# Thin transfers on the GpSimd queue, two weight tiles on the ACT queue, and a new order of the first matmuls, in a decoder-step kernel

## The chip, the cores and the metric

The kernel runs on one core of one Trainium2 chip. The metric is the device time of one execution in microseconds; the median of three timed runs is compared. A core has five instruction queues that run beside each other and wait for one another through semaphores: PE (TensorE, the matrix engine, with its weight loads shown as PEld), DVE (VectorE), ACT (ScalarE), POOL (GpSimd) and SP (SyncE, which computes nothing and here issues transfers). A transfer between device memory (HBM) and the on-chip memory (SBUF) is issued by one of these queues and carried out by 16 DMA engines that the core has. A queue works strictly in order, so what stands in front of an instruction on its queue delays it.

## The reference

One layer of a decoder trunk for 320 tokens (256 of a prompt, and 8 sequences of 8 tokens), with D_MODEL = 2048 and everything in float32:

```python
u = x @ w_in                                              # 2048 x 6680
q, k, v, o_pre, i_pre, f_pre, z, xbc, dt_pre = split_columns(u, SPLIT_SIZES)
h_m, C, n, m = mlstm_mixer(q, k, v, o_pre, i_pre, f_pre, b_i, b_f, m_norm_w, C0, n0, m0)
h_s, S, sconv = ssd_mixer(z, xbc, dt_pre, s_conv_w, s_conv_b, dt_bias, A_log, D_skip, s_norm_w, S0, sconv0)
mix = jnp.concatenate([h_m, h_s], axis=-1) @ w_out        # 2048 x 2048
x = layer_norm(ALPHA * x + mix, ln1_g, ln1_b)
f, fconv = conv_ffn(x, w_up, f_conv_w, f_conv_b, w_down, fconv0)   # 2048 x 11008, 5504 x 2048
x = layer_norm(ALPHA * x + f, ln2_g, ln2_b)
```

The two mixers are recurrences (matrix memory with gates; a state-space model with a short convolution). `conv_ffn` runs a three-tap convolution over the up-projected rows of the tokens, whose last two rows per sequence come in as a state (`state_ffn_conv`) and go out as one (`p_fconv`, `s_fconv`). Outputs are the tokens after the layer and all new states.

## The kernel before, in words

The weights (about 200 MB) pass through SBUF once. `Stream` holds a list of weight tiles in the order of use. A tile is 512 KB, 4 k-tiles of 128 rows by 256 columns. `Stream.load` (its transfers are line L61) issues the next tiles on the SP queue as far as there are free slots: four `raw` slots, and at the very start four more tiles in memory that is used for other things later. `Stream.split_to` writes each quarter of the work as two float32r parts: `hi` on ACT (L74) and `lo = raw - hi` on DVE (L75), five of each ahead. A slot is free again when the `lo` of its last part is done.

`run_groups` issues the products: for every k-tile of a unit of 128 output columns three matmuls of 128x320, `hi` by `XH`, `hi` by `XL` and `lo` by `XH` (all through the helper `mm`, L232). With 4 k-tiles to a quarter a weight tile feeds 24 matmuls. Between the quarters the background work is issued in small steps by `Tasks`: generators that yield an estimated TensorE time in ns before their next step. The order of all queues is written out when the program is built; that estimate alone decides where a step lands among the matmuls.

Three places matter here.

**The start.** `x_load` fetches x and the 128x128 identity on SP. `x_transpose` (through the helper `transpose`, L238) turns a block of x on PE, three transposes to a k-tile, then ACT writes `XH` (L406) and DVE `XL` (L407). Four k-tiles are turned before the first product. `load_small` (L461 to L476) issues 17 thin transfers on SP, norm weights, biases, masks and a convolution state, and about 26 us of PE estimate later transposes some of them. `keep_x` adds `XH` and `XL` on POOL (L420) and multiplies the sums with the gate weights on PE (shown as `bk<-T,T`).

**The out projection.** `out_task` works on each of 16 outputs; its two running sums are additions on POOL (L1390, L1393). `ffn_consts` issues ten transfers on SP: eight of `state_ffn_conv` (L1333), one of the convolution's weights (L1335) and one of its bias (L1336), each 86 partitions wide with rows of 512 bytes; 20 us of estimate later PE transposes them (`bk<-ident,rows`).

**The last down projection.** `fstate` stores the new convolution state in nine transfers on SP (L1516, L1518), `gb_rows` and a line before it load the second norm's weights.

Of the kernel before, what the change touches and what calls it, by code (L numbers as in the profile page):

```python
# [21 lines left out]
class Stream:  # L22
    """Weight tiles: loaded ahead, split into float32r parts hi + lo ahead of the matmuls."""
# [20 lines left out]
    def load(self, upto=None, own=()):  # L44
        """Load ahead, as far as there are slots; own tiles are used before the slots."""
        own = list(own)
        while self.nr < len(self.raws) and (own or self.live < self.RB):
            if upto is not None and self.nr >= upto:
                return
            src = self.raws[self.nr]  # L50
            if own:
                t = own.pop(0)
                self.foreign.add(self.nr)
            else:
                t = self.pool.tile([128, 1024], F32, name=f"raw{self.nr}", tag="raw", bufs=self.RB)
                self.live += 1
            t = t[:, 0:src.shape[1] * src.shape[2]].rearrange("p (k m) -> p k m", m=src.shape[2])
            m = src.shape[2]
            step = m if self.nr else 128
            for c in range(0, m, step):  # L60
                self.nc.sync.dma_start(t[:, :, c:c + step], src[:, :, c:c + step])  # L61
            self.rt[self.nr] = t
            self.nr += 1
# [21 lines left out]
    def get(self, q):  # L85
        self.split_to(q + self.HB - 1)
        return self.got.pop(q)
# [83 lines left out]
def _hybrid_step(ctx, tc, I, O):  # L171
    nc = tc.nc
    V, A, G = nc.vector, nc.scalar, nc.gpsimd
    dma = nc.sync.dma_start
# [32 lines left out]
    class Halves:  # L207
        """16 k-tiles as two tiles of 8, so that the first half is free early."""
# [43 lines left out]
    # ---------------------------------------------------------------- constants  # L252
# [9 lines left out]
    def run_groups(groups, mvh, mvl, kmap, done, budget, before=None, n=NT, mark=None):  # L262
        for us in groups:
            for o in us:
                o.ps = bank()
            for s in range(4):
                for o in us:
# [16 lines left out]
            before = None  # L284
# [4 lines left out]
    def rsqrt(pool, x, eps, shape, step=0):  # L289
        """1 / sqrt(x + eps), elementwise on a small tile; x is overwritten."""  # L290
# [26 lines left out]
    def colbc(dg):  # L317
        """Per-token columns (as diagonals) to a bank with the tokens along the free dim, equal in all partitions."""
# [24 lines left out]
    # ---------------------------------------------------------------- weights in the order of use  # L343
# [30 lines left out]
    # ---------------------------------------------------------------- mixer pool, start  # L374
# [10 lines left out]
    G.memset(ones, 1.0)  # L385

# [70 lines left out]
    def load_small():  # L457
        colsr = mt("T1", [108, 128])
        r = 0
        for name, n in (("ln1_g", 16), ("ln1_b", 16), ("mlstm_norm_w", 8), ("ssm_norm_w", 8)):  # L460
            dma(colsr[r:r + n], I[name][0].rearrange("(k p) -> k p", p=128))  # L461
            r += n
        dma(colsr[48:96], I["ssm_conv_w"][0].rearrange("j (k p) -> (j k) p", p=128))
        dma(colsr[96:108], I["ssm_conv_b"][0].rearrange("(k p) -> k p", p=128))
        dma(gbias[:, 0:4], I["mlstm_b_i"].broadcast_to([128, 4]))
        dma(gbias[:, 4:8], I["mlstm_b_f"].broadcast_to([128, 4]))
        dma(gbias[:, 8:24], I["ssm_dt_bias"].broadcast_to([128, 16]))
        dma(alog, I["ssm_A_log"].broadcast_to([128, 16]))
        dma(bicol, I["mlstm_b_i"].rearrange("o h -> h o"))
        dma(m0, I["state_mlstm_m"][0].rearrange("b h -> h b"))  # L470
        hr = mt("T10", [24, 1536])
        dma(hr, I["state_ssm_conv"][0].rearrange("b r c -> (b r) c"))
        dma(c_tm, I["c_tm"])
        dma(dsk, I["ssm_D"].broadcast_to([128, 16]))
        dma(m01, I["c_m01"])
        dma(sel, I["c_sel"])  # L476
        yield 21000
# [12 lines left out]
    # ---------------------------------------------------------------- gates  # L490
# [14 lines left out]
    def gate_task(pg):  # L505
# [23 lines left out]
        # log1p(e) = 2 atanh(e / (2 + e))  # L529
# [31 lines left out]
        # SSD rows  # L561
# [12 lines left out]
        # mLSTM rows  # L574
# [27 lines left out]
        dma(d_s, wd[32:48])  # L602
        dma(d_b, bs[:, 0:NT])
        dma(d_m, M4)
        dma(d_w, ws)
# [13 lines left out]
        dma(O["p_m"][0].rearrange("b h -> h b"), m4[:, 255:256])  # L619
        dma(O["s_m"][0].rearrange("b h -> h b"), ms)  # L620

    # ---------------------------------------------------------------- conv of x, B, C
# [33 lines left out]
    def conv_state():  # L656
# [9 lines left out]
        dma(O["p_sconv"][0].rearrange("b r c -> (b r) c"), so[0:3])  # L666
        dma(O["s_sconv"][0].rearrange("b r c -> (b r) c"), so[3:27])

    # ---------------------------------------------------------------- SSD
# [27 lines left out]
    def ssd_bc():  # L697
        # sample operands: rows (b, term, t); terms x: h l h l, B: h h l l
# [77 lines left out]
    def ssd_sample():  # L776
        """Sample states: products with C for four sequences at a time in column tiles, then the update in place."""
# [185 lines left out]
    # ---------------------------------------------------------------- mLSTM  # L963
# [36 lines left out]
    def ml_setup():  # L1000
        yield from wait("gates", "ssd")
        n0r = mt("T1", [64, 128])
        dma(n0r, I["state_mlstm_n"][0].rearrange("b h (e p) -> (b h e) p", p=128))
# [5 lines left out]
        dma(mbig, I["c_mbig"])  # L1009
# [35 lines left out]
    def ml_prompt_state():  # L1045
# [30 lines left out]
        dma(O["p_n"][0, 0].rearrange("h (e p) -> (h e) p", p=128), po)  # L1076

    def ml_ops():
        """Per head: stacked float32r parts of k * w and v of the samples, and their sum over time."""
# [43 lines left out]
        dma(O["s_n"][0].rearrange("b h (e p) -> (b h e) p", p=128), no)  # L1123
# [183 lines left out]
    run_groups(in_groups, XH, XL, lambda k: k, in_done, 1300, before=start_x, mark="in")  # L1307
# [21 lines left out]
    def ffn_consts():  # L1329
        yield 25000  # L1330
        hr = fr("rows", [86, 16, 128])
        for b in range(8):
            dma(hr[:, 2 * b:2 * b + 2, :], I["state_ffn_conv"][0, b].rearrange("r (i p) -> i r p", p=128))  # L1333
        wr = fr("rows", [86, 4, 128])
        dma(wr[:, 0:3, :], I["ffn_conv_w"][0].rearrange("j (i p) -> i j p", p=128))  # L1335
        dma(wr[:, 3, :], I["ffn_conv_b"][0].rearrange("(i p) -> i p", p=128))  # L1336
# [117 lines left out]
    # ---------------------------------------------------------------- conv FFN  # L1454
# [50 lines left out]
    def fstate():  # L1505
# [10 lines left out]
        dma(O["p_fconv"][0, 0].rearrange("r (i p) -> i r p", p=128), r[:, 0:2, :])  # L1516
        for b in range(8):
            dma(O["s_fconv"][0, b].rearrange("r (i p) -> i r p", p=128), r[:, 2 * b + 2:2 * b + 4, :])  # L1518
# [36 lines left out]
    def gb_rows():  # L1555
        """The norm's g and b as float32r rows g hi, g lo, g hi, b hi, b lo."""
# [5 lines left out]
        for h in range(2):  # L1562
            s = slice(1024 * h, 1024 * h + 1024)
            t = fr("rx", [5, 1024])
            dma(t[0:3], I["ln2_g"][:, s].broadcast_to([3, 1024]))
            dma(t[3:5], I["ln2_b"][:, s].broadcast_to([2, 1024]))
# [11 lines left out]
    for j in range(3):  # L1578
# [13 lines left out]
        if j == 2:  # L1592
            fin["r01"], r2g = fr("big", [128, 2, D]), fr("big", [128, 2, D])
            fin["r2"], fin["g"] = r2g[0:64, 0, :], r2g[:, 1, :]
            dma(fin["g"], I["ln2_g"].broadcast_to([128, D]))
# [10 lines left out]
    # ---------------------------------------------------------------- second norm  # L1606
    # y = (r g) rs + (g nb + b), with the second term from the tensor engine: nb in two parts times the rows of gb_rows.
# [57 lines left out]
def _constants():  # L1665
    """Identity, causal masks and the cumulative-sum matrix (prompt anchored at token 128, sample per sequence)."""
# [49 lines left out]
```

## Time and profile before

| what | value |
|---|---|
| median of 3 runs | 1589.42 us (1588.61 to 1590.03) |
| span of the profiled execution, first to last instruction | 1583.8 us |
| median less span (launch, what lies around the span) | 5.6 us |
| PE busy | 1550.8 us, 98% of the span |
| DVE, ACT, POOL busy | 969.4, 776.3, 241.8 us |
| bytes moved, mean rate | 253.87 MB, 160 GB/s |
| mean granted TensorE clock | 0.990 |

A row of the timeline reads: start in us, duration in us, engine, line of the kernel, operation, written tile `<-` read tiles with their shapes, and how many neighbours were merged (`x8`). In brackets stands how long the engine had been idle before it and what ended that. Rows of "SPq" are the SP queue issuing a transfer; they last as long as the issue keeps the queue, not as long as the bytes take. The page gives one execution its span and no run time of its own, so the span is set against the median by the 5.6 us of the table.

### The profile page before, as it was taken

The numbers are of one execution on the slowest core, as the hardware profiler recorded it, in microseconds if no ns is written. First come the engines' busy times: TensorE is split into PE (matmuls) and PEld (weight loads), VectorE is DVE, ScalarE is ACT, GpSimd is POOL, SyncE is SP. The second block draws the span as 40 slices with busy tenths as digits, with TensorE's granted clock in tenths as the row PEclk, the third lists the DMA queues.
The fourth block names the chain that finished last, engine by engine and source line by source line (L and its number), as shares of the span: only waits on it lengthen the run. The fifth ranks groups of instructions, "written<-read, shape, count | busy, mean of one in ns | idle before, by whom it ended". The sixth has DMA issues, their size and how long they took to land.

```text
span 1583.8 us, 27952 instructions
## 1 busy us (share of the span) xinstructions
PE 1550.8 (98%) x10533; PEld 1500.2 (95%) x10533; DVE 969.4 (61%) x1957; ACT 776.3 (49%) x1533; POOL 241.8 (15%) x548
## 2 busy tenths in 40 slices
PE   8999999999999989999999999999999999999896
PEld 7999889998889989999999999999999999999896
DVE  4775445655677566687777545655644555656565
ACT  4665333444546435566665435555533555555332
POOL 2212110023301033232331000000000000000001
PEclk9999999999999999999999999999999999999998
DMA  8646665466774625454444454454444445454352
GB/s 220 205 140 160 195 193 172 139 185 198 229 231 150 208 91 192 131 155 150 147 148 141 146 163 151 135 158 147 147 153 154 147 147 160 147 150 164 122 160 79
DMA packets 267523, 253.87 MB, mean 160 GB/s; under 512 B 15987, under 2 KB 262207, under 8 KB 267260
## 3 DMA queue, kind: packets, MB, share of 16 engines
q1 hardware_dynamic: 267388, 252.09, 51.6%
q8 instruction: 82, 1.34, 0.3%
q14 instruction: 53, 0.43, 0.1%
HBM read 231.63 MB, written 20.43 MB: 159 GB/s over the span
## 4 chain that ended last, share of the span: by engine, by line
PE 89%; issue 6%; SPq 3%; DMA 1%; DVE 1%; POOL 0%; ACT 0%; POOLq 0%; ACTq 0%; DVEq 0%
PE bk L232 87%; PE bk L238 2%; SPq L1333 1%; DMA T<-w_in 1%; SPq L445 0%; DMA raw<-w_out 0%; DMA T<-state_ssm_conv 0%; SPq L61 0%; POOL big L1644 0%; SPq L1336 0%; DVE big L1379 0%; DVE lo L75 0%; SPq L1335 0%; SPq L461 0%; DVE big L1383 0%
## 5 line engine op out<-in xcount | busy, mean ns | idle before, releaser
L75 DVE TENSOR_TENSOR lo<-raw,hi 128x512 fp32r<-128x512 f32 (+2 forms) x800 | 551.3, 699 | 420.2 <-ACT hi L74 418.4
L74 ACT ACTIVATE hi<-raw 128x512 fp32r<-128x512 f32 (+2 forms) x800 | 486.4, 616 | 474.3 <-PE bk L232 418.9
L232 PE MATMUL bk<-big,hi 128*128 128x320 f32 (+1 forms) x2752 | 609.3, 310 | 0.0
L232 PEld LDWEIGHTS bk<-big,hi 128*128 128x128 f32 x2752 | 462.3, 188 | 0.2
L232 PE MATMUL bk<-big,lo 128*128 128x320 f32 (+1 forms) x1376 | 426.5, 310 | 0.0
L232 PE MATMUL bk<-XH,hi 128*128 128x320 f32 x832 | 269.2, 324 | 0.0
L232 PEld LDWEIGHTS bk<-big,lo 128*128 128x128 f32 x1376 | 259.3, 188 | 0.0
L232 PE MATMUL bk<-XH,lo 128*128 128x320 f32 x832 | 258.0, 310 | 0.0
L232 PE MATMUL bk<-XL,hi 128*128 128x320 f32 x832 | 257.9, 310 | 0.0
L232 PE MATMUL bk<-HH,hi 128*128 128x320 f32 x688 | 215.2, 313 | 5.0 <-ACT hi L74 5.0
L232 PE MATMUL bk<-HH,lo 128*128 128x320 f32 x688 | 213.5, 310 | 0.0
L232 PE MATMUL bk<-HL,hi 128*128 128x320 f32 x688 | 213.3, 310 | 0.0
L232 PEld LDWEIGHTS bk<-XH,hi 128*128 128x128 f32 x832 | 157.1, 189 | 14.4 <-issue 4.6
L232 PEld LDWEIGHTS bk<-XL,hi 128*128 128x128 f32 x832 | 157.3, 189 | 0.2
L232 PEld LDWEIGHTS bk<-XH,lo 128*128 128x128 f32 x832 | 157.1, 189 | 0.0
L232 PEld LDWEIGHTS bk<-HH,hi 128*128 128x128 f32 x688 | 130.0, 189 | 5.2 <-ACT hi L74 5.2
L1482 DVE SCALAR_TENSOR_TENSOR c<-c,fcol,c 128x336 f32<-128x336 f32 x172 | 98.0, 570 | 58.3 <-ACT c L1480 55.3
L232 PEld LDWEIGHTS bk<-HH,lo 128*128 128x128 f32 x688 | 129.8, 189 | 0.2 <-DVE lo L75 0.2
L232 PEld LDWEIGHTS bk<-HL,hi 128*128 128x128 f32 x688 | 129.9, 189 | 0.0
L193 POOL TENSOR_SCALAR fst<-c 128x18 f32<-128x18 f32 x86 | 22.2, 265 | 567.4 <-ACT c L1475 567.4
L232 PE MATMUL bk<-MH,hi 128*128 128x320 f32 x256 | 80.5, 315 | 10.8 <-ACT hi L74 10.8
L232 PE MATMUL bk<-MH,lo 128*128 128x320 f32 x256 | 79.8, 312 | 0.0
(299 smaller groups left out, 1447.3 us busy)
## 6 DMA issues: line engine op xcount, KB each, us to landing
raw<-ffn_w_up SPq DMA_DIRECT2D x172, 512.0 KB
raw<-w_in SPq DMA_DIRECT2D x100, 512.0 KB
raw<-ffn_w_down SPq DMA_DIRECT2D x71, 512.0 KB
raw<-w_out SPq DMA_DIRECT2D x32, 512.0 KB
T<-state_mlstm_C SPq DMA_DIRECT2D x32, 256.0 KB
s_C<-T SPq DMA_DIRECT2D x32, 256.0 KB
T<-state_ssm SPq DMA_DIRECT2D x8, 512.0 KB
s_ssm<-T SPq DMA_DIRECT2D x8, 512.0 KB
```

Of the source, the lines that this page charges most:

```text
L74: nc.scalar.activation(h, src, AF.Copy)
L75: nc.vector.tensor_tensor(l, src, h.bitcast(F32), ALU.subtract)
L193: G.tensor_scalar(out, in_, 1.0, 0.0, ALU.mult, ALU.add)
L232: nc.tensor.matmul(out, lhsT=lhsT, rhs=rhs, start=start, stop=stop)
L238: nc.tensor.transpose(out, in_, ident[b:b + p, b:b + p])
L1333: dma(hr[:, 2 * b:2 * b + 2, :], I["state_ffn_conv"][0, b].rearrange("r (i p) -> i r p", p=128))
L1482: V.scalar_tensor_tensor(c[:, 0:336], xp[:, j:j + 336], fcol[:, j, i:i + 1], c[:, 0:336], ALU.mult, ALU.add)
```

## The change

Five edits. The thin transfers of `load_small`, `gate_task` (its four scratch stores and two outputs), `conv_state`, `ml_setup` (two), `ml_ops`, the prompt's last state, `ffn_consts`, `fstate`, `gb_rows` and the load of the second norm's g go to the POOL queue (`gdma`); transfers of weights, x, the matrix states and the outputs y stay on SP. The first two weight tiles are issued on ACT. Seven 128x128 products of ones by ones, whose result nobody reads, stand at the head of PE. The first four k-tiles of x are no longer turned in one go: the first products stand between the transposes. And the first call of `get` splits one quarter only, no longer five.

```diff
-                self.nc.sync.dma_start(t[:, :, c:c + step], src[:, :, c:c + step])
+                (self.nc.sync if self.nr > 1 else self.nc.scalar).dma_start(t[:, :, c:c + step], src[:, :, c:c + step])
...
     def get(self, q):
-        self.split_to(q + self.HB - 1)
+        self.split_to(q + self.HB - 1 if q else 0)
...
-    dma = nc.sync.dma_start
+    dma, gdma = nc.sync.dma_start, nc.gpsimd.dma_start
...
                     for kk in range(nk):
                         k = k0 + kk
+                        if each is not None:
+                            each(us.index(o), s, kk)
...
     G.memset(ones, 1.0)
+    warm = bank()
+    for _ in range(7):
+        mm(warm[:, 0:128], ones, ones, True, True)
...
-    def x_transpose(c):
-        flags.add(("xt", c))
-        t = box.pop(("x", c))
-        for kk in range(4):
+    def x_transpose(c, kks=range(4)):
+        t = box["x", c]
+        if kks[-1] == 3:
+            flags.add(("xt", c))
+            del box["x", c]
+        for kk in kks:
...
-            if k == 1:
-                st.split_to(0)
...
     def load_small():
+        yield 9000
...
-            dma(colsr[r:r + n], I[name][0].rearrange("(k p) -> k p", p=128))
+            gdma(colsr[r:r + n], I[name][0].rearrange("(k p) -> k p", p=128))
...
-        dma(sel, I["c_sel"])
-        yield 21000
+        gdma(sel, I["c_sel"])
+        yield 17000
...
         if u == s == 0:
-            x_transpose(0)
+            x_transpose(0, [0])
...
+    def each_x(u, s, kk):
+        if u == s == 0 and kk < 3:
+            x_transpose(0, [kk + 1])
...
-            dma(hr[:, 2 * b:2 * b + 2, :], I["state_ffn_conv"][0, b].rearrange("r (i p) -> i r p", p=128))
+            gdma(hr[:, 2 * b:2 * b + 2, :], I["state_ffn_conv"][0, b].rearrange("r (i p) -> i r p", p=128))
...
-            dma(O["s_fconv"][0, b].rearrange("r (i p) -> i r p", p=128), r[:, 2 * b + 2:2 * b + 4, :])
+            gdma(O["s_fconv"][0, b].rearrange("r (i p) -> i r p", p=128), r[:, 2 * b + 2:2 * b + 4, :])
```

Where the instructions stand now (the changed file's lines are up to 10 higher than the old ones):

On SP in the out projection, before: loads of `w_out` into `raw` slots, with the ten transfers of `ffn_consts` (into `rows`) among them.

```order
L61 DMA raw_6529<-w_out 128x4x256
L61 DMA raw_6577<-w_out 128x4x256
L1333 DMA rows_6628<-state_ffn_conv 86x2x128 x8
L1335 DMA rows_6637<-ffn_conv_w 86x3x128
L1336 DMA rows_6637<-ffn_conv_b 86x128
L61 DMA raw_6644<-w_out 128x4x256
```

Now the ten are gone from SP, and stand on POOL between the additions of `out_task`, behind the sixth pair of them (`c_6271` and `c_6272` are the two running sums):

```order
L1400 TENSOR_TENSOR c_6271<-c_6271,big_6268 128x320
L1403 TENSOR_TENSOR c_6272<-c_6272,c_6629 128x320
L1343 DMA rows_6636<-state_ffn_conv 86x2x128 x8
L1345 DMA rows_6645<-ffn_conv_w 86x3x128
L1346 DMA rows_6645<-ffn_conv_b 86x128
L1400 TENSOR_TENSOR c_6271<-c_6271,big_6268 128x320
L1403 TENSOR_TENSOR c_6272<-c_6272,c_6668 128x320
```

What stands behind them on POOL are the remaining additions. On the matrix engine the place of the transposes of `rows` did not move.

On POOL at the start, now: the 17 transfers of `load_small` stand between the last memset and the additions of `keep_x` (`T_51`, `T_52`), which before followed that memset at once. The rows show the first two of the 17 and the last two.

```order
L940 MEMSET sm_201 128x6
L467 DMA T_49_291<-ln_g 16x128
L467 DMA T_49_291<-ln_b 16x128
...
L481 DMA T_18_130<-c_m 128x448
L482 DMA sel<-c_sel 128x128
L425 ISA
L425 TENSOR_TENSOR T_51_344<-XH_162,XL_164 128x640
L425 TENSOR_TENSOR T_52_346<-XH_162,XL_164 128x640
```

So the additions, and the gate products on PE that read them, now come behind 17 issues on POOL.

On PE at the start, now (before, all twelve transposes `ident,T` came first):

```order
L232 MATMUL bk_80<-ones 128x128 x7
L238 MATMUL bk_158<-ident,T_3_89 128x128 x2
L238 MATMUL bk_158<-ident,T_2_88 128x64
L238 MATMUL bk_170<-ident,T_3_89 128x128 x2
L238 MATMUL bk_170<-ident,T_2_88 128x64
L232 MATMUL bk_154<-XH_162,hi_166 128x320
L232 MATMUL bk_154<-XL_164,hi_166 128x320
L232 MATMUL bk_154<-XH_162,lo_167 128x320
L238 MATMUL bk_179<-ident,T_3_89 128x128 x2
L238 MATMUL bk_179<-ident,T_2_88 128x64
```

The products of the first k-tile moved ahead of the transposes of the third, and need `lo_167` from DVE there.

More of the change, by code (lines that the diff above doesn't have):

```diff
@@ L260, in col, with run_groups @@
         return cols[:, i:i + 1]
-    def run_groups(groups, mvh, mvl, kmap, done, budget, before=None, n=NT, mark=None):
+    def run_groups(groups, mvh, mvl, kmap, done, budget, before=None, n=NT, mark=None, each=None):
         for us in groups:
@@ L283, in run_groups @@
                     tasks.pump(budget)
-            before = None
+            before = each = None
     def ktiles(w, k, n, c, m):
@@ L460, in load_small @@
         for name, n in (("ln1_g", 16), ("ln1_b", 16), ("mlstm_norm_w", 8), ("ssm_norm_w", 8)):
-            dma(colsr[r:r + n], I[name][0].rearrange("(k p) -> k p", p=128))
+            gdma(colsr[r:r + n], I[name][0].rearrange("(k p) -> k p", p=128))
             r += n
[L463 to L470, printed above, removed]
-        hr = mt("T10", [24, 1536])
[L472 to L476, printed above, removed]
-        yield 21000
+        gdma(colsr[48:96], I["ssm_conv_w"][0].rearrange("j (k p) -> (j k) p", p=128))
+        gdma(colsr[96:108], I["ssm_conv_b"][0].rearrange("(k p) -> k p", p=128))
+        gdma(gbias[:, 0:4], I["mlstm_b_i"].broadcast_to([128, 4]))
+        gdma(gbias[:, 4:8], I["mlstm_b_f"].broadcast_to([128, 4]))
+        gdma(gbias[:, 8:24], I["ssm_dt_bias"].broadcast_to([128, 16]))
+        gdma(alog, I["ssm_A_log"].broadcast_to([128, 16]))
+        gdma(bicol, I["mlstm_b_i"].rearrange("o h -> h o"))
+        gdma(m0, I["state_mlstm_m"][0].rearrange("b h -> h b"))
+        hr = mt("T10", [24, 1536])
+        gdma(hr, I["state_ssm_conv"][0].rearrange("b r c -> (b r) c"))
+        gdma(c_tm, I["c_tm"])
+        gdma(dsk, I["ssm_D"].broadcast_to([128, 16]))
+        gdma(m01, I["c_m01"])
+        gdma(sel, I["c_sel"])
+        yield 17000
         ps = bank()
@@ L601, in gate_task @@
         yield 9000
[L602 to L605, printed above, removed]
+        gdma(d_s, wd[32:48])
+        gdma(d_b, bs[:, 0:NT])
+        gdma(d_m, M4)
+        gdma(d_w, ws)
         p1 = bank()
@@ L618, in gate_task @@
         yield
-        dma(O["p_m"][0].rearrange("b h -> h b"), m4[:, 255:256])
-        dma(O["s_m"][0].rearrange("b h -> h b"), ms)
+        gdma(O["p_m"][0].rearrange("b h -> h b"), m4[:, 255:256])
+        gdma(O["s_m"][0].rearrange("b h -> h b"), ms)
     XS = mt("T10", [128, 8, NT])
@@ L665, in conv_state @@
         yield
-        dma(O["p_sconv"][0].rearrange("b r c -> (b r) c"), so[0:3])
-        dma(O["s_sconv"][0].rearrange("b r c -> (b r) c"), so[3:27])
+        gdma(O["p_sconv"][0].rearrange("b r c -> (b r) c"), so[0:3])
+        gdma(O["s_sconv"][0].rearrange("b r c -> (b r) c"), so[3:27])
     def ssd_cb():
@@ L1008, in ml_setup @@
         mbig = mt("T2", [128, 448])
-        dma(mbig, I["c_mbig"])
+        gdma(mbig, I["c_mbig"])
         wb = sm([128, 4, 72], name="wb")
@@ L1122, in ml_ops @@
         yield
-        dma(O["s_n"][0].rearrange("b h (e p) -> (b h e) p", p=128), no)
+        gdma(O["s_n"][0].rearrange("b h (e p) -> (b h e) p", p=128), no)
     def ml_chunks():
@@ L1306, in _hybrid_step @@
         tasks.add(t)
-    run_groups(in_groups, XH, XL, lambda k: k, in_done, 1300, before=start_x, mark="in")
+    run_groups(in_groups, XH, XL, lambda k: k, in_done, 1300, before=start_x, mark="in", each=each_x)
     first = []
@@ L1332, in ffn_consts @@
         for b in range(8):
-            dma(hr[:, 2 * b:2 * b + 2, :], I["state_ffn_conv"][0, b].rearrange("r (i p) -> i r p", p=128))
+            gdma(hr[:, 2 * b:2 * b + 2, :], I["state_ffn_conv"][0, b].rearrange("r (i p) -> i r p", p=128))
         wr = fr("rows", [86, 4, 128])
-        dma(wr[:, 0:3, :], I["ffn_conv_w"][0].rearrange("j (i p) -> i j p", p=128))
-        dma(wr[:, 3, :], I["ffn_conv_b"][0].rearrange("(i p) -> i p", p=128))
+        gdma(wr[:, 0:3, :], I["ffn_conv_w"][0].rearrange("j (i p) -> i j p", p=128))
+        gdma(wr[:, 3, :], I["ffn_conv_b"][0].rearrange("(i p) -> i p", p=128))
         yield 20000
@@ L1564, in gb_rows @@
             t = fr("rx", [5, 1024])
-            dma(t[0:3], I["ln2_g"][:, s].broadcast_to([3, 1024]))
-            dma(t[3:5], I["ln2_b"][:, s].broadcast_to([2, 1024]))
+            gdma(t[0:3], I["ln2_g"][:, s].broadcast_to([3, 1024]))
+            gdma(t[3:5], I["ln2_b"][:, s].broadcast_to([2, 1024]))
             yield 6000
```

8 lines of the change are left out of this document (4 added, 4 removed).

## The prediction

> **What bounds the kernel now.** I read the page's head first, then the busy time and granted clock in stretches of 10 us, and then the timeline of each stretch where PE was not full.
>
> ```profile
> span 1583.8 us, 27952 instructions
> PE 1550.8 (98%) x10533; PEld 1500.2 (95%) x10533; DVE 969.4 (61%) x1957; ACT 776.3 (49%) x1533; POOL 241.8 (15%) x548
> 580.00:590.00 10.00, 6.38 (x44) 6.11 (x42) 0.39 (x1) 0.00 (x0) 0.00 (x0) 1.00 0.15 38
> 590.00:600.00 10.00, 2.82 (x10) 2.60 (x11) 2.67 (x4) 3.50 (x8) 1.92 (x2) 0.52 0.81 268
> 628.84 825.17 PE bk L232 x5604
> ```
>
> PE is the bound almost everywhere: what the change does under a full PE is worth nothing, and only the 33 us in which PE is not busy can be won. The stretch rows (busy time of PE, PEld, DVE, ACT, POOL, then clock, DMA share, GB/s) show one hole: from 580 to 600 PE works 9.2 of 20 us. Other holes lie at 1495, in the first 6 us and in the last 20. The change does not touch the last. The last row, from the chain of waits, gives the pace of a full PE: 825.17 / 5604 = 0.147 us for a matmul.
>
> The two holes in the middle, on PE and on ACT, which makes the `hi` that PE waits for:
>
> ```profile
> 586.07 0.31 PE L232 MATMUL bk<-MH,lo 128*128 128x320 f32 x1
> 597.18 0.63 PE L232 MATMUL bk<-MH,hi 128*128 128x320 f32 x1 [10.80 <-ACT hi L74]
> 600.66 0.31 PE L232 MATMUL bk<-MH,hi 128*128 128x320 f32 x1
> 596.50 0.63 ACT L74 ACTIVATE hi<-raw 128x512 fp32r<-128x512 f32 x1 [17.27 <-DMA raw<-w_out]
> 1495.44 0.31 PE L232 MATMUL bk<-HH,lo 128*128 128x320 f32 x1
> 1500.71 0.63 PE L232 MATMUL bk<-HH,hi 128*128 128x320 f32 x1 [4.96 <-ACT hi L74]
> 1505.07 0.32 PE L232 MATMUL bk<-HH,hi 128*128 128x320 f32 x1
> 1500.03 1.98 ACT L74 ACTIVATE hi<-raw 128x512 fp32r<-128x512 f32 x4 [12.78 <-DMA raw<-ffn_w_down]
> ```
>
> ACT waited for a weight tile both times. Why the tile was late stands on the SP queue:
>
> ```profile
> 561.64 6.08 SPq L61 DMA_DIRECT2D raw<-w_out  x2
> 567.77 16.38 SPq L1333 DMA_DIRECT2D rows<-state_ffn_conv  x8
> 584.20 2.31 SPq L1335 DMA_DIRECT2D rows<-ffn_conv_w  x1
> 586.55 3.31 SPq L1336 DMA_DIRECT2D rows<-ffn_conv_b  x1
> 589.96 2.96 SPq L61 DMA_DIRECT2D raw<-w_out  x3
> 1477.57 15.82 SPq L1518 DMA_DIRECT2D s_fconv<-rows  x8
> 1493.51 16.02 SPq L61 DMA_DIRECT2D raw<-ffn_w_down  x8
> ```
>
> Ten thin transfers kept SP from 567.77 to 589.9; then three tiles went out at once, so slots had been free. Eight stores kept it from 1477.57 to 1493.4. The queue was the bound there, while the DMA engines were 15% busy (580 to 590).
>
> **The change, part by part.** The sum is made on the profiled execution, 1583.8 us of span; the median of 1589.42 lies 5.6 us above it, and I take those as unchanged.
>
> *First hole.* With the ten gone from SP, tile loads follow the slots. At 0.147 us the next matmul was due at 586.22 and came at 597.18: 10.96 us. Then 12 matmuls, 597.18 to 600.66, took 3.48 us at the low clock against 12 x 0.147 = 1.76: 1.72 more. Term: -12.7.
>
> *Second hole.* 1495.59 to 1500.71 is 5.12; 15 matmuls to 1505.07 took 4.36 against 2.20: 2.16. Term: -7.3. On POOL the nine stores hold up nobody:
>
> ```profile
> 1446.06 0.11 POOL L1611 MEMSET fsm<- 128x15 f32 x1
> 1574.01 5.15 POOL L1644 TENSOR_TENSOR big<-big,rx 64x512 f32<-64x512 f32 x4 [127.83 <-ACT rx L1643]
> ```
>
> POOL is idle for 127.8 us, and the 14 transfers that now fall in there (norm rows too) fit at any price below 9 us each.
>
> *The price of an issue on POOL* is not in this trace: all its transfers are SP's. The nearest rows:
>
> ```profile
> 26.48 1.07 SPq L461 DMA_DIRECT2D T<-ln_g  x1
> 33.80 0.43 SPq L476 DMA_DIRECT2D sel<-c_sel  x1
> L1333 SPq DMA_DIRECT2D rows<-state_ffn_conv x8: 359/2308/3798, 567.8 to 581.8; - x8
> ```
>
> The 17 of `load_small` took SP 26.48 to 34.23, 0.46 us each; the eight of `state_ffn_conv` took 0.36 at best and 2.31 at the median. So 0.46 to 2.31 for either kind. I take 1.0 for the 17, the middle of the bounds as a ratio, since these very transfers are the low row; and 1.3 for the ten, which carry more rows (172 of 512 bytes each). Nothing excludes the ends.
>
> The Trainium skill ("DMA: Bandwidth & Descriptors", Latency and other measured facts) puts the first byte at about 1 us from the GpSimd queue and 0.6 from SP. Here no run shows the first; by 1.0 us for all 27 the sum would come out the same.
>
> The same page (Issuing engines are not separate DMA queues) speaks against the change: all queues share 16 DMA engines, and issuing from several saves only issue time, usually small beside the transfer. The trace differs: 22 us of issue beside idle DMA engines. By the rule the two terms would be nothing, which is the last rival below; I go by the rows.
>
> *Where POOL's issues could come through to PE.* First the out projection: the ten stand behind the sixth pair of sums, and PE transposes `rows` later.
>
> ```profile
> 0.73 0.45 SPq L393 DMA_DIRECT2D T<-x_prompt  x1
> 571.31 0.91 POOL L1393 TENSOR_TENSOR c<-c,c 128x320 f32<-128x320 f32 x1
> 602.42 0.46 PE L238 MATMUL bk<-ident,rows 86*128 86x86 f32 x4
> ```
>
> That addition is the sixth and ends at 572.2. PE gets to the transposes 24 matmuls behind the hole, without it at 586.22 + 24 x 0.147 = 589.75. Landing takes some 2.5 us (an estimate from the first x tile, 256 KB, issued at 0.73 and used by PE at 4.09, a row further down: 3.4 in all). So 572.2 + 10p + 2.5 must stay under 589.75: p up to 1.5 us is hidden. At 1.3 it is, by 2 us: cost 0. Behind the ten on POOL wait the other sums; what reads those comes after the sixteenth output, and `c` has nine buffers beside the sums, so this costs nothing; if that cover were gone, the price is the 13 us.
>
> Second, the start, where `keep_x`'s additions now stand behind 17 issues:
>
> ```profile
> 2.40 0.10 POOL L934 MEMSET sm<- 128x6 f32 x1
> 7.89 4.06 POOL L420 TENSOR_TENSOR T<-XH,XL 128x640 f32<-128x640 f32 x2 [5.39 <-DVE XL L407]
> 29.72 0.74 PE L232 MATMUL bk<-T,T 128*32 128x320 f32 x8
> ```
>
> POOL is free at 2.5, two additions take 4.06, and PE wants them at 29.7, or 28.7 with what the start gains. 2.5 + 17p + 4.06 stays below that up to p = 1.3. At 1.0 they are done at 23.6: cost 0, with 5 us of cover. The stores of these sums wait on SP with weight loads behind them, in time with the same additions: no further cost.
>
> *The other thin transfers* (states, gate rows, `mbig`) are 12 of about 1 us each, spread from 120 to 540 us, where PE is full and POOL 15% busy overall; four tiles ahead, 14 us of matmuls, hide a late SP row behind them. 0; without cover some 2 us at each.
>
> *The start.*
>
> ```profile
> 4.09 0.66 PE L238 MATMUL bk<-ident,T 128*128 128x128 f32 x2 [4.09 <-DMA ident<-c_ident]
> 5.54 3.10 PE L238 MATMUL bk<-ident,T 64*128 64x64 f32 x10 [0.78 <-DMA T<-x_sample]
> 8.57 0.63 PE L232 MATMUL bk<-XH,hi 128*128 128x320 f32 x1
> 13.51 0.31 PE L232 MATMUL bk<-XH,hi 128*128 128x320 f32 x1
> 16.15 2.31 PE L238 MATMUL bk<-ident,T 128*128 128x128 f32 x12
> 543.43 0.70 PE L232 MATMUL bk<-big,ones 128*128 128x320 f32 x2
> 5.94 0.44 ACT L406 ACTIVATE XH<-bk 128x320 fp32r<-128x320 f32 x1 [3.92 <-PE bk L238]
> 2.97 1.57 SPq L61 DMA_DIRECT2D T<-w_in  x3
> ```
>
> Nothing on PE can start before 4.09, the identity's landing, so the seven products of ones are free: by the row at 543.43 (about 0.55 us for 320 columns at the high clock) 128 columns cost 0.22, or 0.43 at the low clock, 3.0 us for seven, from 0.9 to 4. The three issues on ACT (1.57) fit into its 3.92 idle. What can be won is the slow clock: 18 products took 8.57 to 13.51, 4.9 us, where 18 x 0.147 is 2.6: 2.3. Ten transposes took 3.10, 0.31 each, where twelve later ones took 2.31, 0.19 each: 1.4 for twelve. At most 3.7. On the other side, weight tiles now share the DMA engines with x from the first moment; x_sample, ahead of them so far, may land up to 1 us later. And each early product waits for ACT and DVE (`XH`, then `hi` of 0.63, then `lo`) between transposes, where nothing waited before; if the clock rises no earlier, some 0.8 us are lost. So -3.7 to +1.8; I take -1.0, half the products' part.
>
> The clock rose at 13.5, 4.9 us after the first product, though PE had transposed since 5.5. The Trainium skill ("TensorE: Matmul & The Clock Gate", Part 4: PE-mode transpose) says transposes do not count as busy in the same way; the trace agrees. Its Part 1 asks for about 3.4 us of sustained matmuls: by an estimate from that figure 3.0 us of ones fall just short and the term would be nearer +1 than -1.
>
> Sum: 1583.8 - 12.7 - 7.3 - 1.0 = 1562.8 of span, 1568.4 at the median.
>
> **Rivals.**
> - *POOL is slow for the ten.* At 2.0 us each the transposes wait 572.2 + 20 + 2.5 - 589.75 = 5.0 us, and a pause like that of 1495 costs 2.2 of clock: 1575.6. For it: the 2.31 median. Against: on SP those were back to back, with the first at 0.36. Chance 0.18.
> - *The ten's bytes, not the queue, hold up the tiles of the first hole.* It stays, at 1581.1. For it: the eight got slower after the first (0.36 to 2.31). Against: 15% DMA share, 38 GB/s. Chance 0.04.
> - *POOL at the start.* At 1.6 us each for the 17, the gate products wait 2.5 + 27.2 + 4.06 - 28.7 = 5.1: about 1573.5. Chance 0.06.
> - *Slower than before:* every issue on POOL costs like SP's slow ones, and PE stands behind both groups. The loss is 17p - 22.1 and 10p - 15.0; with 21.0 gained it decides from p = 2.15. At 2.31 it is 17.2 + 8.1 - 21.0 = +4.3: 1593.7. Against: SP issued the 17 at 0.46. Chance 0.04.
> - *The change does not do what it says:* the same DMA engines hold up the tiles at both holes whichever queue issues, and only the start gains: 1588.4. Three tiles went out at once behind the first block, so 0.04.
>
> The forecast has 0.64, with 1565.5 to 1571 of its own (start term -3.7 to +1.8). The range goes up through the two POOL cases: 1565.5 to 1580. Three runs of this kernel spread 0.1%, so 0.2%, 3.2 us, is what a comparison can tell. Faster takes the forecast and the first three rivals: 0.92; slower 0.04; same, the last rival, 0.04.
>
> **What would show it.** No idle row of PE near 586 or 1495, and the clock at 1.00 from 580 to 610; SP's loads of `w_out` 3.5 us apart there; POOL's ten issues ending before 587; the gate products at 28 to 30 without a wait. Products of 0.15 us spacing before 10 us would show the start's term. A wait of PE's transposes for `rows`, or of `bk<-T,T` for POOL, would prove me wrong, and its length is the price I mis-sized.

## The result, and the profile after

| | kernel before | changed kernel |
|---|---|---|
| median of the runs compared, us | 1589.01 (1586.03 to 1590.03) | 1578.95 (1578.14 to 1580.12) |
| ratio, 95% interval | | 0.9945, 0.9933 to 0.9957 |
| profiled execution, span, us | 1583.8 | 1578.3 |

The change gains 10.1 us by the medians; the ratio of 0.9945 puts the gain at 0.55%. The forecast was 1568.4, a gain of 21. The page of the changed kernel, its head:

```profile
span 1578.3 us, 27987 instructions
PE 1553.8 (98%) x10547; PEld 1502.5 (95%) x10547; DVE 976.6 (62%) x1957; ACT 773.1 (49%) x1532; POOL 290.3 (18%) x601
```

PE still fills 98%. The stretches of 10 us show where it does not (after the length of the stretch: busy time of PE, PEld, DVE, ACT, POOL, then granted clock, DMA share, GB/s):

```profile
580.00:590.00 10.00, 10.00 (x70) 10.00 (x69) 7.00 (x12) 5.17 (x10) 10.00 (x7) 1.00 1.03 212
590.00:600.00 10.00, 3.83 (x27) 3.56 (x25) 4.85 (x2) 1.78 (x3) 6.48 (x8) 0.85 1.26 181
600.00:610.00 10.00, 7.91 (x42) 7.90 (x43) 3.86 (x8) 2.38 (x5) 1.19 (x1) 0.64 0.41 114
...
1490.00:1500.00 10.00, 10.00 (x72) 9.99 (x71) 5.94 (x17) 3.49 (x6) 0.00 (x0) 1.00 0.47 150
```

The hole at 1495 is gone. The hole near 590 has only moved by some 7 us, and the DMA share in it is now 1.26 (590 to 600); the old hole began with a share of 0.15. The timeline of the changed kernel there, PE, POOL and the SP queue:

```profile
593.52 0.31 PE L232 MATMUL bk<-MH,lo 128*128 128x320 f32 x1
602.09 0.83 PE L238 MATMUL bk<-ident,rows 86*128 86x86 f32 x4 [8.27 <-DMA rows<-ffn_conv_w]
607.30 0.31 PE L232 MATMUL bk<-MH,lo 128*128 128x320 f32 x1
...
576.06 12.80 POOL L1343 DMA_DIRECT2D rows<-state_ffn_conv  x8
588.85 1.84 POOL L1345 DMA_DIRECT2D rows<-ffn_conv_w  x1
590.69 0.56 POOL L1346 DMA_DIRECT2D rows<-ffn_conv_b  x1
...
583.19 14.26 SPq L61 DMA_DIRECT2D raw<-w_out  x4
```

PE no longer waits for a weight tile. It waits for the thin rows themselves: POOL has issued the last of the ten by 591.25, before PE's last product, but `ffn_conv_w` lands 13.2 us after its issue. The DMA view of 560 to 606 gives KB and the median time from issue to landing:

```profile
raw<-w_out SPq DMA_DIRECT2D x10, 512.0 KB, 8.4
rows<-state_ffn_conv POOLq DMA_DIRECT2D x8, 86.0 KB, 11.4
rows<-ffn_conv_w POOLq DMA_DIRECT2D x1, 129.0 KB, 13.2
```

From the first issue, 576.06, to the last landing, 602.25 in the trace, are 26.2 us. On SP the ten had held the queue for 22.1, and their last packet ended 26.6 us after the first issue (567.77 to 594.35 in the packet records). The time is nearly the same, on another queue. The weight tiles suffer with them: 8.4 us from issue to landing here, against 3.9 at the median of all `w_out` tiles of this kernel.

**Where the 5.4 us between the two spans come from.** The first row of the table is PE's first gate product, the third a product of PE. The others are the split (`lo`) of one and the same weight tile, in both traces, us:

| place | before | after | shift |
|---|---|---|---|
| gate products, start | 29.72 | 32.57 | +2.85 |
| a tile ahead of the first hole | 575.65 | 578.57 | +2.9 |
| the last product ahead of that hole in the kernel before | 586.07 | 590.00 | +3.93 |
| a tile behind it | 631.18 | 633.24 | +2.05 |
| a tile ahead of the second hole | 1448.18 | 1450.23 | +2.05 |
| a tile behind it | 1542.27 | 1537.02 | -5.25 |

The splits run ahead of PE, so a shift that PE has just taken does not show in them yet. By PE's own products the start costs 2.5 (at 543 in the kernel before). Another 1.4 comes soon behind that, in a stretch with this row of the changed kernel:

```profile
548.10 0.41 PE L232 MATMUL bk<-MH,lo 128*128 128x320 f32 x1 [0.68 <-DVE lo L75]
```

The kernel b_cut below, whose code up to there is that of the kernel before, loses 1.2 at the same place, so the change need not be the cause. The first hole then gives 3.93 - 2.05 = 1.9 and the second 7.3. The first products and what is around them, in the changed kernel on PE and POOL:

```profile
0.99 3.36 PE L232 MATMUL bk<-ones 128*128 128x128 f32 x14 [0.99 <-POOL ones L387]
5.46 0.66 PE L238 MATMUL bk<-ident,T 128*128 128x128 f32 x2 [1.11 <-DMA ident<-c_ident]
7.42 1.27 PE L238 MATMUL bk<-ident,T 64*128 64x64 f32 x4 [1.29 <-DMA T<-x_sample]
8.83 0.64 PE L232 MATMUL bk<-XH,hi 128*128 128x320 f32 x1
9.99 0.93 PE L238 MATMUL bk<-ident,T 128*128 128x128 f32 x3
10.84 0.63 PE L232 MATMUL bk<-XH,hi 128*128 128x320 f32 x1
11.81 0.93 PE L238 MATMUL bk<-ident,T 128*128 128x128 f32 x3
16.82 0.30 PE L232 MATMUL bk<-XH,hi 128*128 128x320 f32 x1
...
32.57 0.75 PE L232 MATMUL bk<-T,T 128*32 128x320 f32 x8
...
2.44 0.68 POOL L467 DMA_DIRECT2D T<-ln_g  x1
8.86 0.54 POOL L473 DMA_DIRECT2D gbias<-ssm_dt_bias  x1 [2.07 <-DMA T<-ln_g]
15.25 3.11 POOL L425 TENSOR_TENSOR T<-XH,XL 128x640 f32<-128x640 f32 x2
```

The identity is there at 5.46 where it was there at 4.09, and `x_sample` is transposed at 7.42, 1.88 later than before, so the first product does not come earlier although only half the transposes stand ahead of it; the other six now stand between the products, 0.85 us for each group of three; and the spacing drops to 0.15 us only at 16.8, not at 13.5. POOL issues the 17 in 0.51 to 0.68 us each and is at its sums by 15.25, so it holds up nothing.

### The profile page after: what moved, and what is told of

It reads as the page before. It is cut to its first block, busy times and chain, and to the rows that moved or that the text cites. A ratio compares the mean times of both kernels' runs of the same rounds, so it can differ in the third digit from the quotient of the medians.

```text
span 1578.3 us, 27987 instructions
## 1 busy us (share of the span) xinstructions
PE 1553.8 (98%) x10547; PEld 1502.5 (95%) x10547; DVE 976.6 (62%) x1957; ACT 773.1 (49%) x1532; POOL 290.3 (18%) x601
## 4 chain that ended last, share of the span: by engine, by line
PE 86%; issue 7%; DMA 2%; POOL 1%; DVE 1%; ACT 1%; POOLq 0%; SPq 0%; DVEq 0%; ACTq 0%
PE bk L232 84%; PE bk L238 2%; DMA rows<-ffn_conv_w 1%; POOL T L425 1%; DMA raw<-w_out 1%; DVE lo L75 1%; DMA T<-ln_g 0%; DMA gbias<-ssm_dt_bias 0%; DMA xT<-T 0%; POOL big L1654 0%; ACT hi L74 0%; DVE big L1393 0%; DVE big L1389 0%; ACT L657 0%; ACT T L644 0%
```

## Experiments on the first hole

Theory A says that the ten transfers run over few DMA engines. Rivals: POOL's queue is slow by itself (B); the weight tiles set the stop (C).

**r_cut: the same rows, cut at partition 80.**

```
-        for b in range(8):
-            gdma(hr[:, 2*b:2*b+2, :], state_ffn_conv[0, b] "r (i p) -> i r p")
-        gdma(wr[:, 0:3, :], ffn_conv_w) ; gdma(wr[:, 3, :], ffn_conv_b)
+        for s in (slice(0, 80), slice(80, 86)):
+            gdma(hr[s], state_ffn_conv[0] "b r (i p) -> i (b r) p" [s])
+            gdma(wr[s, 0:3, :], ffn_conv_w [s]) ; gdma(wr[s, 3, :], ffn_conv_b [s])
```

> The changed kernel with the thin loads of ffn_consts still on POOL, the same rows of 512 bytes, but cut by partitions into 80 and 6 (and the eight of state_ffn_conv put together, so six transfers instead of ten). Theory A, few DMA engines: while only these transfers ran in the kernel before, the DMA share was 0.15 of 16 engines, 2.4 engines, and 172 rows took 2.31 us; in the changed kernel they landed at the same pace, 23 us for all, whichever queue issued them. The Trainium skill (DMA: Bandwidth & Descriptors, How many engines) says that the number of partitions decides, 86 giving 2 engines and 80 giving 16. By A the rows land within 5 us of their issue, the 8.27-us wait of PE for rows and the slow clock behind it (together 11.8 us) are gone: about 1567 us, 12 below the changed kernel. Rival B, POOL's queue itself is slow (its issue of 1.59 us, its landing of 11 us): the rows land as late as now, PE waits 6 to 8 us, 1576 to 1579.

Measured: 1568.4 us, ratio 0.9883 (0.9867 to 0.9900), span 1565.4. Its stretch, its timeline (POOL, PE) and its DMA view:

```profile
590.00:600.00 10.00, 10.00 (x74) 9.99 (x73) 8.15 (x14) 5.62 (x11) 3.39 (x4) 1.00 0.59 182
```

```profile
573.94 0.99 POOL L1344 DMA_DIRECT2D rows<-state_ffn_conv  x1
574.93 0.66 POOL L1345 DMA_DIRECT2D rows<-ffn_conv_w  x1
577.38 0.55 POOL L1346 DMA_DIRECT2D rows<-ffn_conv_b  x1
591.53 0.46 PE L238 MATMUL bk<-ident,rows 86*128 86x86 f32 x4
```

```profile
rows<-state_ffn_conv POOLq DMA_DIRECT2D x1, 640.0 KB, 7.7
rows<-ffn_conv_b POOLq DMA_DIRECT2D x1, 40.0 KB, 9.0
```

The wait and the slow clock are gone: the span is 13.0 us shorter than the changed kernel's, and the median 10.6. Of the 13.0, 2.1 stand ahead of the hole already (the product at 586.07 in the kernel before is at 587.86 here, a shift of 1.79 against 3.93); the hole itself accounts for 10.8. B falls: the queue is the same. From the first issue, 573.94, to the last landing, 585.36, are 11.4 us in place of 26.2. The landing in 7.7 to 9.0 us is more than the 5 that A said; that miss costs nothing, since PE comes at 591.5. The packet records show the spread that A needs: in the kernel before, from 576 to 585, on average 2.4 of these packets were in flight and never more than 4; in r_cut, from 574 to 580, 8.2 on average and up to 19. POOL's packets are larger, though, mostly 4 KB where SP's have 512 bytes; the comparison on one queue with one packet size follows with b_cut. The Trainium skill (DMA: Bandwidth & Descriptors, Why a DMA increments its semaphore by 16 and not by 1, on how many engines) says the transfer is split over the largest number up to 16 that divides its partition counts, which makes 2 for 86 and 16 for 80. The 2.4 packets on SP agree; the page names exceptions for some copies from the GpSimd queue, and the packet records do not name the engine.

**r_early: uncut, but issued long before.**

```
-        yield 25000      (ahead of the ten)
+        yield 8000
-        yield 20000      (ahead of their transposes)
+        yield 38500
```

> The changed kernel with the ten thin loads, uncut, issued some 17 to 24 us earlier, the transposes at the same matmul. Theory A, few engines: the ten take 23 us to land from about 552 to 560, so they are there by 584, before PE's transposes at 593.5, and the wait for rows is gone; weight tiles that share their engines land up to 16 us after issue, where four slots cover some 14, so PE may lose 0 to 3 us to hi instead: 1567 to 1570. Rival C, the place of the stop is set by the weight tiles that land late, and the rows are only the last to be seen: PE stops 8 us for hi in place of rows, 1576 to 1579.

Measured: 1576.87 us, ratio 0.9929 (0.9914 to 0.9944). POOL came to them much earlier than I had worked out, 55 us before the changed kernel and not 17 to 24:

```profile
520.76 12.77 POOL L1343 DMA_DIRECT2D rows<-state_ffn_conv  x8 [4.53 <-DVE lo L75]
535.36 0.57 POOL L1346 DMA_DIRECT2D rows<-ffn_conv_b  x1
551.58 1.68 DVE L1376 SCALAR_TENSOR_TENSOR big<-rx,bk 128x320 f32<-128x320 f32 x4 [11.21 <-DMA rx<-xT]
552.17 1.41 PE L232 MATMUL bk<-big,ones 128*128 128x320 f32 x2 [5.20 <-issue]
```

The ten again take 25.2 us from first issue to last landing (545.94), and now the x rows of the first norm (`rx`) land late behind them: DVE waits 11.2 us, PE stops for 5.2 and then runs at the low clock. A had the pace right and the price wrong (0 to 3 us forecast, some 8 measured); C, a stop for `hi`, did not happen either. The stop went to the reader that was due in those 25 us.

**b_cut: the kernel before, all on SP, loads cut as in r_cut and the eight stores of `s_fconv` made two.**

```
+        for s in (slice(0, 80), slice(80, 86)):
+            dma(s_fconv[0] "b r (i p) -> i (b r) p" [s], r[s, 2:18, :])
```

> The kernel before, everything still on SP; only the loads of ffn_consts are cut into 80 and 6 partitions (the eight of state_ffn_conv together, six transfers for ten) and the eight stores of s_fconv are made two in the same way. Theory A, few DMA engines: SP is held for some 3 to 6 us instead of 22 and 16, both holes are gone without any other queue: 1583.8 - 12.7 - 7.3 = 1563.8 of span, about 1569. Rival B2, it is SP as the queue of weight tiles that must not have thin transfers at all (the number of rows counts, 1720 and 1376, not the engines): the holes stay, 1585 to 1589.

Measured: 1567.59 us, ratio 0.9877 (0.9862 to 0.9892), span 1565.4; run again as the base of a later group, 1566.13, 0.9862 (0.9848 to 0.9877). Its SP queue:

```profile
569.31 0.50 SPq L1334 DMA_DIRECT2D rows<-state_ffn_conv  x1
569.86 0.67 SPq L1335 DMA_DIRECT2D rows<-ffn_conv_w  x1
572.01 0.29 SPq L1336 DMA_DIRECT2D rows<-ffn_conv_b  x1
575.85 3.24 SPq L61 DMA_DIRECT2D raw<-w_out  x3
...
1466.69 4.69 SPq L1518 DMA_DIRECT2D s_fconv<-rows  x2
```

SP is held for 3.0 us instead of 22.1, and for 5.1 (with `p_fconv`) instead of about 16. Both holes are gone without any other queue. This is faster than the kernel before and than the changed one. The shift of PE against the kernel before goes from +1.79 (the product at 586.07) to -10.89 (the one at 635.60), which is 12.7, and the tiles then go from -10.88 near 1448 to -18.19 near 1542, which is 7.3: the two terms of the prediction.

On the same queue and with the same packets of 512 bytes, 16.2 are in flight on average (571.5 to 576.2, up to 27) where it was 2.4. All 1720 rows run from their first packet to their last in 4.6 us instead of 24.4.

**f_pool: the changed kernel with its start undone, `load_small` back on SP, loads and stores cut but still on POOL.**

> The changed kernel with its start undone and load_small on SP (both as before), the loads of ffn_consts and stores of s_fconv still on POOL, but cut as in b_cut. If the queue is worth nothing once the transfers are cut: within 0.1% of b_cut, spans within 1 us. If freeing SP is worth something by itself: 1 to 3 us less.

Measured: 1566.65 us, ratio 0.9864 (0.9849 to 0.9878), beside 1566.13 for b_cut on the same chip, with spans of 1564.5 and 1565.7: no difference that these runs can tell. Once the transfers are cut, POOL's queue is worth nothing here. In all these runs the eight transfers of `state_ffn_conv` were merged as well as cut. The transfer of `ffn_conv_w` was only cut: POOL's issue of it fell from 1.84 us to 0.66 and 0.58 for its two pieces, and SP's from 2.31 to 0.67 and 0.52. In the kernel before the last 344 rows, which are those of `ffn_conv_w` and `ffn_conv_b`, took 4.9 us by themselves, more than all 1720 together in b_cut. So the cut alone has this effect; what the merging adds was not measured.

## Experiments on the second hole and on the start

**b_stores: the kernel before, only the nine stores of `fstate` on POOL.**

> The kernel before with only the nine stores of fstate on POOL. By the second term of the prediction, which the changed kernel's trace gives as 7.33 us of shift between the tiles near 1448 and 1542: 1583.8 - 7.3 = 1576.5 of span, about 1582, ratio 0.9954. Rival: the gain there came with the changed order of the rest, 1586 to 1589.

Measured: 1579.99 us, ratio 0.9958 (0.9943 to 0.9973). In its trace the tile shift goes from +4.29 near 1448 to -3.00 near 1542: 7.29, the term of the prediction (the 7.33 in the expectation is 7.30 by the table above). The +4.29 ahead of it is a surprise, since nothing there was edited. In this kernel's trace and in that of the kernel before, from 40 to 46 us:

```profile
40.00:46.00 6.00, 6.00 (x25) 4.50 (x25) 2.35 (x4) 1.58 (x3) 0.00 (x0) 0.50 1.02 354
```

```profile
40.00:46.00 6.00, 6.00 (x45) 5.29 (x44) 2.10 (x4) 2.65 (x6) 1.09 (x2) 1.00 1.04 367
```

Behind 24 transposes that start at 36.8 (36.4 before) the clock is granted at 0.50 in the one execution and at 1.00 in the other. In b_cut's second trace it fell at the same place for 3.4 us. In the other traces it stayed up there, or fell only behind an idle row of PE of 2.2 us or more (s_sp and f_ones below). The same code thus costs up to 3.3 us more or less, from one execution to the next.

**The start, one piece undone at a time.** The changed kernel with the two tiles back on SP (s_sp), with the first tile's transposes in one go (s_block), with `load_small` back on SP (s_small), without the ones (s_noones):

```
s_sp:      -(sync if nr > 1 else scalar).dma_start    +sync.dma_start
s_block:   -x_transpose(0, [0]), each_x, get's "if q else 0"    +x_transpose(0), split_to(0) at k == 1
s_small:   -gdma(...) x17, yield 9000 / 17000    +dma(...) x17, yield 21000
s_noones:  -for _ in range(7): mm(warm[:, 0:128], ones, ones, True, True)
```

> The changed kernel with the first two weight tiles back on SP, all else kept. Theory D, the tiles take the DMA engines from x at the start: x_sample lands near 5.5 again instead of 7.4, the first product comes at 7.0 to 7.6 instead of 8.83 and the gate products at about 31 instead of 32.57: 1.5 us gained. Rival E, the 17 thin transfers from POOL delay x_sample: it still lands at 7.0 to 7.6, first product at 8.6 to 9.5, gate products at 32 to 33.5, no gain.

> The changed kernel with the transposes of the first tile of x in one go ahead of the products again, all else kept. Theory F, transposes between the first products hold the clock low for one 3.4-us window longer: the products run without a break from about 10.4, the clock rises near 13.5, and the gate products come at 31 to 31.7 instead of 32.57. Rival G, only the late landing of x_sample counts: the clock rises one window after the first unbroken products, near 16.8 as now, and the gate products come at 32.3 to 33.

> The changed kernel with the 17 thin loads of load_small back on SP at their old place, all else kept. Theory E, they share the DMA engines in the first 15 us and make x_sample late: it lands at 6.5 or before instead of 7.4, and the gate products come at 30.5 to 31.5 instead of 32.57. Theory D, only the two tiles of the ACT queue make it late: x_sample still lands at 7.2 to 7.5, first product near 8.8, gate products at 32 to 33.

> The changed kernel without the seven products of ones. If they do nothing (the clock in the changed kernel rose at 16.7, behind 25 slow products): same first product, the clock rises between 13.4 and 16.8 as the windows fall, gate products within 0.5 us of 32.57. If they were of use: the clock rises one window of 3.4 us later, gate products near 34.

| kernel | `x_sample` transposed | first product | clock rises for good | gate products | ratio (95%) |
|---|---|---|---|---|---|
| before | 5.54 | 8.57 | 13.5 | 29.72 | |
| changed | 7.42 | 8.83 | 16.7 | 32.57 | 0.9945 (0.9933 to 0.9957) |
| s_sp | 4.95 | 7.90 | 13.6 | 34.22 | 0.9960 (0.9949 to 0.9971) |
| s_block | 7.63 | 11.24 | 14.2 | 32.35 | 0.9951 (0.9936 to 0.9965) |
| s_small | 7.27 | 8.59 | 14.9 | 31.64 | 0.9953 (0.9938 to 0.9968) |
| s_noones | 7.20 | 8.61 | 16.7 | 32.44 | 0.9951 (0.9934 to 0.9967) |

None makes a difference in time that its interval can tell. The traces tell more. D has the landing right: with the tiles on SP, `x_sample` is there at 4.95, and with `load_small` on SP it still comes at 7.27, so E falls as its cause. All traces of this case agree: 7.12 to 7.63 in the seven with the two tiles on ACT, 4.94 to 6.19 in the seven with them on SP. But D's gain does not arrive, in s_sp:

```profile
7.90 0.63 PE L232 MATMUL bk<-XH,hi 128*128 128x320 f32 x1 [1.67 <-ACT hi L74]
34.22 1.29 PE L232 MATMUL bk<-T,T 128*32 128x320 f32 x8 [2.18 <-DMA T<-w_in]
```

The product starts 0.9 earlier and PE then waits 2.2 us for the gate weights. The DMA engines are full from 10 to 20 us, in the kernel before as well (the share adds up the time of packets, and comes out above 1):

```profile
10.00:20.00 10.00, 10.00 (x56) 9.06 (x55) 6.87 (x11) 5.21 (x10) 3.56 (x3) 1.00 1.09 321
```

In s_block:

```profile
11.24 0.63 PE L232 MATMUL bk<-XH,hi 128*128 128x320 f32 x1
14.27 0.30 PE L232 MATMUL bk<-XH,lo 128*128 128x320 f32 x1
32.35 0.74 PE L232 MATMUL bk<-T,T 128*32 128x320 f32 x8 [0.80 <-DMA T<-w_in]
```

F is right on the clock: with unbroken products it rises 3 us after the first of them. One trace would not show this, since the rise falls differently in each execution, but all of them together do: 2.6 to 5.8 us after the first product in the six traces with unbroken products and no ones between the transposes, 5.7 to 8.4 us in the seven with transposes between the products. In time F is wrong: the gate products come where G put them. They gain 1.0 and give 0.8 of it back at the same gate weights. The ones do nothing that lasts: without them the clock rises at the same 16.7; with them three of the traces (s_block, s_small, r_cut) show one spell of 3.4 us at full clock from 3.9 to 5.0 on, and then 6.8 us at half.

**f_start and f_ones: on the base of b_cut, the change's start, and a start in which PE never rests.** f_start takes over all edits of the start but one (`load_small` stays on SP); f_ones keeps b_cut's start and adds:

```
+    warm_up(7)                      (seven products of ones, ahead)
+            if c == 0: warm_up(2)   (two more behind each k-tile's transposes)
```

> b_cut with the start of the changed kernel (first two weight tiles from the ACT queue, seven products of ones, transposes between the first products; load_small stays on SP). If the start of the change costs what its trace shows: gate products at 31.5 to 32.6 instead of 30.1, and 1.5 to 2.5 us more than b_cut. If the later stages take such a shift up: gate products late all the same, but the end within 0.7 us of b_cut.

> b_cut with seven products of ones ahead of the transposes and two more behind each of the first four k-tiles' transposes, so that PE never rests from 1.0 us on; tiles and transposes as before. If the clock goes by how full PE's windows of 3.4 us are with products: it rises near 4.5 to 8 and stays, the 18 slow products and the slow transposes go, 1.5 to 2.5 us less than b_cut, gate products at 27.6 to 28.6. If transposes between them keep it low: it rises near 13.5 as now, gate products at 30 to 31.

f_start: 1568.2 us, 0.9874 (0.9860 to 0.9889), beside 1566.13 for b_cut in the same group; gate products at 32.15 against 29.62. By the medians the start of the change costs about 2 us, and later stages do not take it up. The evidence is weaker than for the holes: the two intervals overlap, and the two traced spans differ by 0.6 only (1566.3 and 1565.7), since b_cut's trace, the slowest of its four executions, has the fall of the clock near 40 us and f_start's has not.

f_ones: 1568.07 us, 0.9870 (0.9853 to 0.9887): no gain. In its trace:

```profile
9.32 0.31 PE L232 MATMUL bk<-XL,hi 128*128 128x320 f32 x1
29.32 0.74 PE L232 MATMUL bk<-T,T 128*32 128x320 f32 x8 [0.82 <-DMA T<-w_in]
36.21 1.29 PE L238 MATMUL bk<-ident,T 24*128 24x24 f32 x12 [2.34 <-DMA T<-state_ssm_conv]
```

The clock does what was expected: the clock record shows full clock from 5.7, and products are 0.15 us apart from 10.05 on. The gain is lost at the next landings, 0.8 us at the gate weights and 2.3 at `state_ssm_conv`, and behind the second wait the slow clock is back, from 36.4 to 43.2. Moving those two transfers ahead as well was not tried.

## Why the prediction was wrong

*What bounds the kernel, second hole (-7.3): right.* The shift across it is 7.30 in the changed kernel and 7.29 with that edit alone; the nine stores hold up nobody on POOL.

*First hole (-12.7): the step that failed is "Landing takes some 2.5 us", and with it the reading that "the queue was the bound there".* POOL's price was near: 1.59 for each of the eight, 1.84 and 0.56 for the last two, 15.2 us for the ten where I took 13. POOL was free 3.9 us later than in the trace of before, at 576.06, but PE was later by the same 3.9: 576.06 + 15.2 + 2.5 = 593.8, and PE was due at 593.67. The issues fit. The landings did not, 11.4 to 13.2 us instead of 2.5. I took the landing from a 128-partition tile at the start; its row gives 3.4 us from issue to use, and what PE waited for there was the identity. Even the cut rows of r_cut, spread over more engines, took 7.7 to 9.0 us at this place, so 2.5 was too small for any transfer from POOL there; the few engines explain the rest of the landing and part of the issue time. PE stopped for 602.09 - 593.67 = 8.4 us, and the 17 products from 602.65 to 607.30 cost 4.65 - 17 x 0.147 = 2.15 more. Together 10.6 against the old 12.7, so the term was worth about 2 (1.9 by PE's shift). The price of the hole itself was right: with cut rows the same 12.7 were won.

I had the evidence in a quoted row and read it the wrong way round. A DMA share of 0.15 while SP pushed thin transfers back to back at 2.31 us each did not say that the engines were idle and the queue slow. It said that 2.4 engines of 16 were busy and that SP waited for these: in the packet records 172 rows take 2.33 us, the pace of SP's issues, and with the rows cut SP was held for 3.0 us in all. The rival on that place (the ten's bytes hold up the tiles, 0.04) had the right resource; it was dismissed on this very row. The quoted rule of the Trainium skill (DMA: Bandwidth & Descriptors, Issuing engines are not separate DMA queues) was set aside for it too; f_pool and b_cut, equal in time, bear the rule out at this hole. At the second hole the other queue did help, since nobody waited for the stores to land and the tiles had SP to themselves; cut, the stores could stay on SP.

*Start (-1.0, bounds -3.7 to +1.8): wrong in sign and outside its bounds, +2.85 at the gate products.* Three parts, from the two timelines: the first product 0.26 later; six transposes moved between products, 2 x 0.85 = 1.70; the 36 products up to the next transposes (before 8.57 to 16.15, after 8.83 to 19.02) 10.19 - 1.70 - 7.58 = 0.91 longer. The sum is 2.87. The step named "x_sample ... may land up to 1 us later" was 1.88, and that took away the earlier first product which should have paid for the moved transposes. The price of those, as a cost behind the first product, was missing from the upper bound. The estimate from the Trainium skill (TensorE: Matmul & The Clock Gate, Part 1), by which 3.0 us of ones fall short and the term is nearer +1 than -1, was better than my choice: the ones ran 3.36 us, and in the changed kernel's trace the clock did not rise behind them. In three of the seven traces with these seven ones ahead and no more it did, for one spell of 3.4 us.

*POOL's price for the 17 (1.0 taken): 0.51 to 0.68 measured*, with waits for landings of at most 2.07 between. Cost 0, as forecast. The 12 transfers in the middle: no new idle row of PE by them, as forecast.

*The base, and luck in the number.* I put the median 5.6 us above the profiled span and carried that over. In the later runs of the kernel before, the time is about 2.0 above the same execution's span, and these spans are 1584.1 to 1589.4: the traced execution, at 1583.8, was a quick one. That of the changed kernel, at 1578.3, was the slowest of its four. This is why the medians differ by 10.1 us and the two spans by 5.4. A part may be the clock behind the 24 transposes at 36 us, which b_stores' trace shows fall; how often that happens in the kernel before is not known. On the spans the forecast was 1562.8, 15.5 too low: 10.8 at the first hole (12.7 - 1.9), 3.5 at the start by PE's shift, and 1.4 near 546 that no term had (together 15.7; the spans differ by 0.2 more than the tiles). On the medians it was only 10.5 too low, because 5.6 us were added where about 2 belong. That part was luck. The range up to 1580 holds the measured 1578.95, but it went up there for a POOL that is slow to issue. The first rival named the right wait, that of PE's transposes for `rows`, and the last sentence of the prediction named it as the sign of being wrong; the cause was the landing. (From the start term's bounds the forecast's own range is 1565.7 to 1571.2, where 1565.5 to 1571 was written.)

## What to carry to other kernels

- The queue here that issued thin transfers back to back at a steady 2.31 us each, beside a low DMA share, was held by the few engines that they used. Where a profile looks like this, count the engines first (share x 16), and try to cut the partition count into a multiple of 16 and a rest; that gave here the 20 us of both holes, and moving the transfers to another queue gave 9 of them (1.9 and 7.3).
- A transfer that is moved off a queue still has its landing time. If somebody waits for the landing, sum issue, pace on its engines and landing against the reader's due time; if nobody waits (stores), the other queue is enough.
- At a start where the DMA engines are full (share 1.09 from 10 to 20 us before), look at what lands next before moving products ahead. In the three traces here with an earlier product, an earlier clock or both (s_sp, s_block, f_ones), PE stood for the next transfers and lost 0.8 to 3.2 us in it.

## What had not been expected of the hardware

- Transfers of 86 partitions from SP: 172 rows of 512 bytes in 2.31 us, with 2.4 packets in flight. From POOL all 1720 rows took nearly as long, 22.0 us from the first packet to the last against 24.4. Cut into 80 and 6 they held SP for 3.0 us.
- POOL's issue has two prices here: 0.51 to 0.68 us for the transfers of `load_small`, 1.59 for 172 rows of 86 partitions (0.56 for 86 rows); the cut transfer of 80 partitions and 1280 rows took 0.99.
- POOL's ninth transfer waited 2.07 us for the landing of the first, the tenth 0.62 for that of the second: it had eight under way.
- Towards the end of the thin rows from POOL the weight packets of 1 KB took 104 ns in the median (592 to 601), against 46 ahead of them (560 to 566) and 51 as they began (576 to 592), and tiles landed 8.4 us after issue. Why all tiles slow down, and not only the share on a few engines, these runs do not settle.
- The granted clock moved in spells of 3.4 us or multiples of it: rises at 3.9 to 5.0 that last 3.4, falls of 3.4, 6.8 and 10.2.
